# Spreading the plain units over the chains of a seven-product matrix product, with other lead times for its loads and sums

## The chip, the cores and the metric

The kernel runs on one core of a Trainium2 chip. The core has a matrix engine (TensorE, in profiles PE, with PEld for its weight loads), a vector engine (VectorE, DVE), a scalar engine (ScalarE, ACT), a general one (GpSimd, POOL) and a queue engine (SyncE, SP) that only issues transfers. POOL issues transfers too, here those that add to what is already in on-chip memory. The engines run side by side and wait for one another through semaphores; each takes its own instructions in order.

The metric is the device time of one execution in microseconds (us), the median of three runs.

## The reference

One layer of a hybrid decoder for 512 tokens of width 1024 in fp32: three token mixers, merged by gates, and then a gated MLP with a causal depthwise convolution of width 3, with a residual, and a last RMSNorm. What matters here is the MLP, of inner width 3072:

```python
h2 = rms_norm(x, norm_ffn[l])
up = causal_dwconv(h2 @ w_up[l], ffn_conv_w[l], ffn_conv_b[l])
gate_h, val_h = jnp.split(up, 2, axis=-1)
x = x + (jax.nn.gelu(gate_h, approximate=True) * val_h) @ w_down[l]
...
return rms_norm(x, final_norm)
```

## The kernel before

**fp32 by three passes.** Each operand of a large product is split into a high part, rounded to the matrix engine's fp32r (ACT, L97), and a low part, the rest (DVE, L98). `mm3` (L100) multiplies high by high, high by low and low by high into the same PSUM bank. So each tile of weights and activations is first "split", on ACT and then on DVE, before PE may use it.

**The MLP's tiles.** The inner width is 24 blocks of 128 channels. For each block there is a gate half and a value half. A *plain unit* of the up product (`up_units`) makes one half of one block for all 512 tokens: 24 matmuls. It fetches 512 KB of `w_up` into a buffer of the tag `raw` (three of them, `NRAW`), splits it into buffers `whi` and `wlo` (four of each, `NWB`), multiplies, and evacuates the bank: L1172 on ACT and L1174 twice on DVE are the convolution, and behind the second half of a block L1186 and L1187 are gelu and the product of both halves (`up_mix`). The result `acts[i]` takes a slot of the pool `apool`, tag `s`, which has 51 slots (`NSLOT`) of 2 KB a partition for everything of this size. I call the two units of block 21 up21.0 and up21.1. Some other blocks go through `up_fast`, which is not touched.

**The down product.** Blocks 0 to 19 are multiplied with `w_down` in five groups p of four blocks, each as a product of 2 x 2 parts, by seven products in place of eight (`down_fast`, which builds the operands, and `seven`, which builds the work). The seven products, called a1, a2, c1, c2, b1, b2 and b3, run in this order, each with five *chain units* p = 0 to 4 of 12 matmuls (b2.3 is the unit p = 3 of b2). They need sums of weight parts and of activation parts:

- *Weights.* The part B11 is loaded once per group (two transfers of 256 KB by SP, L296, into two slots of tag `s`) for a1, and stays. Before c1, b1 and b3 another part (B12, B22, B21) is added to it in place, by two accumulating transfers on POOL (L301; I call them sums). b2 loads B12 into two more slots (L296), and adds B22 to it (L301). a2 and c2 use B21 and B22 as they are, through `raw` (`direct`, L305). Each unit's weights are then split into `whi` and `wlo`.
- *Activations.* DVE forms the sums for b1, c1 and c2 (`sum2`, `sum1`, `sum4`; L1317, L1323, L1328). `act_ready` splits a unit's activations into two slots of tag `s`.
- *Banks.* a1, b1, b2 and b3 accumulate in the same two banks, one after the other, and c1 and c2 in two others. At the end of each of these products DVE adds the banks to the residual (`put`, L1341: two instructions), and the next product of the same banks can only go on behind that.

Blocks 20 to 23 are multiplied plainly in the end (`down_units` with `wdown2`: 96 matmuls, with activations split by the steps `halves`), and the last norm follows.

**What sets the order.** `unit`, `made_unit` and `step` put units and steps on a list. Each unit has preparations with a lead, in units: a preparation with lead m is called just ahead of the unit m places earlier (`emit`, L183). The lead counts all units, chain and plain alike; splits have 2 (`AHEAD`). In `seven`, the sums of c1, b1 and b3 have the lead `more`, the loads of b2 the first number of `late`, and its sums the second:

```python
"b1": ("B11", [(more, lambda p: add("B11", "B22", p))]),
"b2": ("B12", [(late[0], lambda p: load("B12", p)), (late[1], lambda p: add("B12", "B22", p))]),
"b3": ("B11", [(more, lambda p: add("B11", "B21", p))]),
```

A planner then makes each engine's queue from this program: an instruction can go ahead of earlier ones of the program when its data and a buffer are there.

When the down product begins, seven plain units are left (up20.1 to up23.1: `us`). The order is written out in the last lines of the kernel: up20.1, a1.0 to a1.4, up21.0, a2.0 to a2.4, up21.1, c1.0 to c1.2, up22.0, c1.3, c1.4, c2.0, c2.1, up22.1, c2.2 to c2.4, up23.0, b1.0 to b1.3, up23.1, b1.4, b2.0 to b2.4, b3.0 to b3.4, with the four `halves` steps in front of b3.0 to b3.3.

Of the kernel before, what the change touches and what calls it, by code (L numbers as in the profile page):

```python
# [34 lines left out]
NF = FF // P  # L35
# [22 lines left out]
def trunk(ctx: ExitStack, tc: tile.TileContext, x, xT, mem, memT, par, wdecay, wch, wv, wg, wmk,  # L58
# [17 lines left out]
    def fslot(shape=(P, S)):  # L76
        return apool.tile(list(shape), F32, tag="s", name=nm("f"))

    def rslot(shape=(P, S)):
        return apool.tile(list(shape), F32R, tag="s", name=nm("r"))  # L80
# [14 lines left out]
    def split(hi, lo, src, eng=None):  # L95

        nc.scalar.activation(hi, src, AF.Copy)  # L97
        return (eng or nc.vector).tensor_tensor(out=lo, in0=src, in1=hi.bitcast(F32), op=ALU.subtract)  # L98
# [34 lines left out]
    def unit(dram, n, fn, parts=1):  # L133

        w = {}
        i = sum(1 for k, *_ in prog if k == "unit")

        def ready():
            w["w"] = fetch(dram, n, parts)
            for h in behind.get(i, ()):  # L140
                h()
        prog.append(("unit", [(AHEAD, ready)], lambda: fn(w["w"])))

    def made_unit(pre, fn):

        prog.append(("unit", pre, fn))

    def step(fn):
        prog.append(("step", [], fn))
# [197 lines left out]
    def run(*parts):  # L347

        for p in parts:
            if isinstance(p, tuple):  # L350
                unit(*p)
            else:
                for v in p:
                    made_unit(*v) if isinstance(v, tuple) else step(v)
# [742 lines left out]
    def gain_rows(src):  # L1097
        for j in range(2):
            gb[j] = fslot()
            with tc.issue_after(loads[-1].ins):  # L1100
                nc.sync.dma_start(gb[j], src[:, j * HB:(j + 1) * HB])

    msq, queue, late = {}, [], []
# [86 lines left out]
    def up_units(tiles, keep, early=0):  # L1190

        us = []
        first = []
        for n in range(2 * len(tiles)):
            i, half = tiles[n // 2], n % 2
            if n < early:

                def fn(w, n=n):
                    first.append((w, channel_major(w, KD, h2k, 0, S // 2)))
                    if n != 1:  # L1200
                        norm2_flip(2 + n // 2)
                    if n == early - 1:
                        for m, (v, ps) in enumerate(first):
                            channel_major(v, KD, h2k, S // 2, S, ps)
                            up_done(ps, tiles[m // 2], m % 2, keep)
                us.append((wup[NF * half + i], D, fn, 2))
            else:
                us.append((wup[NF * half + i], D,
                           lambda w, i=i, half=half: up_done(channel_major(w, KD, h2k), i, half, keep)))
        return us  # L1210
# [92 lines left out]
    def down_fast(np):  # L1303

        a_in, a_sp = {}, {}
        sub, add = ALU.subtract, ALU.add

        def parts(p):

            for key, odd, r in (("a1", 0, 0), ("b2", 0, 1), ("a2", 1, 0), ("b3", 1, 1)):  # L1310
                a_in[key, p] = [acts[4 * p + 2 * j + odd][:, r * HT:(r + 1) * HT] for j in range(2)]


        def sum2(p):
            s2 = a_in["b1", p] = fslot((P, 2, HT))
            for j in range(2):
                nc.vector.scalar_tensor_tensor(out=s2[:, j, :], in0=a_in["b2", p][j], scalar=-1.0, in1=a_in["b3", p][j],  # L1317
                                               op0=ALU.mult, op1=sub)

        def sum1(p):  # L1320
            a_in["c1", p] = a_in["a1", p]
            for j, a in enumerate(a_in["a1", p]):
                nc.vector.tensor_tensor(out=a, in0=a, in1=a_in["b1", p][:, j, :], op=add)  # L1323

        def sum4(p):
            a_in["c2", p] = a_in["a2", p]
            for j, a in enumerate(a_in["a2", p]):
                nc.vector.tensor_tensor(out=a, in0=a, in1=a_in["b1", p][:, j, :], op=add)  # L1328

        def act_ready(key, p):  # L1330
            hi, lo = rslot((P, 2, HT)), rslot((P, 2, HT))
            a = a_in[key, p]
            if isinstance(a, list):
                for j in range(2):
                    split(hi[:, j, :], lo[:, j, :], a[j])
            else:
                split(hi, lo, a)
            a_sp[key, p] = hi, lo

        def put(t, c, src, op=ALU.add):  # L1340
            nc.vector.tensor_tensor(out=x2[t][c], in0=x2[t][c], in1=src, op=op)  # L1341

        def read(key, i, ps):
            put(*{"a1": (i, 0, ps), "a2": (i, 0, ps), "c1": (2 + i, 1, ps), "c2": (i, 1, ps), "b1": (i, 1, ps, sub),
                  "b2": (2 + i, 1, ps, sub), "b3": (2 + i, 0, ps)}[key])

        pre = {k: [(2, lambda p, k=k: act_ready(k, p))] for k in ("a1", "a2", "c1", "c2", "b1", "b2", "b3")}

        pre["a1"].append((3, parts))
        pre["a2"].append((np - 1, sum2))  # L1350
        pre["c1"].append((np - 1, sum1))
        pre["c2"].append((np, sum4))
        return seven(lambda q, p: wdown[p, int(q[1]) - 1, int(q[2]) - 1], HB, np,
                     lambda key, p, j, i: tuple(a[:, j, i * P:(i + 1) * P] for a in a_sp[key, p]), pre, read,
                     chained=True, more=8, late=(8, 5))

    def final_left(t):

# [40 lines left out]
    def halves(i):  # L1399
        a, acts[i] = acts[i], (rslot(), rslot())  # L1400
        split(*acts[i], a)

    us = up_units((0, 1, 2), whole, 3)
# [4 lines left out]
    us = up_units((5, 8, 11, 14, 17, 19), whole) + up_units(range(20, NF), whole)  # L1408
    ahead = None
    for i, even in zip((3, 4, 6, 7, 9, 10, 12, 13, 15, 16, 18), (None, 0, 2, None, 4, 6, 8, 10, 12, 14, None)):  # L1410
# [7 lines left out]
        ahead = f  # L1418
    run([ahead["b1"]], us.pop(0), [lambda: down_s3(16)], [ahead["b2"]], us.pop(0), [ahead["b3"]], [lambda: down_s3(18)])
    down, n = down_fast(5), 0  # L1420
    for m, u in zip((5, 5, 3, 4, 3, 4), us):
        run(u, down[n:n + m])
        n += m
    run(us[-1], down[n:n + 6])
    for i, u in zip(range(20, NF), down[n + 6:]):
        run([lambda i=i: halves(i)], [u])
    run(down[n + 10:])
    step(lambda: gain_rows(gfin))
    weave(down_units(wdown2, lambda k: acts[20 + k], final, None, final_left, 2), [])

# [92 lines left out]
```

## Time and profile before

| | us |
|---|---|
| median of 3 runs | 929.19 (928.91 to 930.28) |
| the profiled execution | 931.17 |
| its span, first to last instruction | 929.1 |
| PE busy | 909.7 |
| DVE busy | 662.1 |
| ACT busy | 537.7 |
| POOL busy | 145.6 |

The profile is of one execution. Its page lists each engine's busy time, the span in 40 slices, the chain of work that ended last, and the costliest groups of instructions by line, tile names and shapes. Other views of the same trace group the instructions by window, list who waited for whom, or give the instructions in order of time. Times in them are counted from the span's start. The down product of blocks 0 to 19 lies at about 763 to 900 us, the plain one of blocks 20 to 23 behind it, up to 922. "POOL f L301" is an issue of a sum, "SPq L296" one of a load, and "ACT whi L97" and "DVE wlo L98" are the two halves of a weight split.

### The profile page before, as it was taken

The numbers are of one execution on the slowest core, as the hardware profiler recorded it, in microseconds if no ns is written. First come the engines' busy times: TensorE is split into PE (matmuls) and PEld (weight loads), VectorE is DVE, ScalarE is ACT, GpSimd is POOL, SyncE is SP. The second block draws the span as 40 slices with busy tenths as digits, with TensorE's granted clock in tenths as the row PEclk, the third lists the DMA queues.
The fourth block names the chain that finished last, engine by engine and source line by source line (L and its number), as shares of the span: only waits on it lengthen the run. The fifth ranks groups of instructions, "written<-read, shape, count | busy, mean of one in ns | idle before, by whom it ended". The sixth has DMA issues, their size and how long they took to land.

```text
span 929.1 us, 13271 instructions
## 1 busy us (share of the span) xinstructions
PE 909.7 (98%) x4786; PEld 790.8 (85%) x4786; DVE 662.1 (71%) x1195; ACT 537.7 (58%) x936; POOL 145.6 (16%) x188
## 2 busy tenths in 40 slices
PE   9999999999999999999999999999999999999796
PEld 7899788888889998888888798999999988888585
DVE  6996855665688567747776668778787789876665
ACT  7775655685855468484534455665565565455544
POOL 0010000000233430330000000222222121306102
PEclk9999999999999999999999999999999999999799
DMA  7446223213468783321157324767676766869602
GB/s 249 141 137 206 91 87 100 88 45 116 115 162 184 173 208 117 111 85 52 52 170 244 112 58 114 183 141 200 141 200 137 175 142 163 166 186 233 137 23 91
DMA packets 55505, 128.55 MB, mean 138 GB/s; under 512 B 6624, under 2 KB 14480, under 8 KB 55440
## 3 DMA queue, kind: packets, MB, share of 16 engines
q1 hardware_dynamic: 37088, 94.99, 31.2%
q0 software_dynamic: 18208, 32.46, 20.5%
q8 instruction: 37, 0.61, 0.3%
q10 hardware_dynamic: 144, 0.26, 0.1%
q14 instruction: 28, 0.23, 0.1%
HBM read 123.23 MB, written 3.67 MB: 137 GB/s over the span
## 4 chain that ended last, share of the span: by engine, by line
PE 77%; issue 7%; DMA 7%; DVE 5%; ACT 2%; POOL 2%; SPq 0%; DVEq 0%; POOLq 0%; ACTq 0%
PE mm L104 65%; PE sm L104 7%; DMA f<-in_wdown 3%; DMA f<-in_wv 2%; PE mm L439 2%; DMA raw<-in_wup 2%; POOL f L301 2%; DVE wlo L98 1%; DVE r L98 1%; ACT r L97 0%; PE sm L999 0%; ACT whi L97 0%; PE sm L986 0%; PE sm L1013 0%; DMA raw<-in_wch 0%
## 5 line engine op out<-in xcount | busy, mean ns | idle before, releaser
L98 DVE TENSOR_TENSOR wlo<-raw,whi 128x1024 fp32r<-128x1024 f32 (+3 forms) x132 | 145.3, 1104 | 86.1 <-ACT whi L97 49.2
L97 ACT ACTIVATE whi<-raw 128x1024 fp32r<-128x1024 f32 (+3 forms) x132 | 125.1, 953 | 127.5 <-PE mm L104 93.2
L104 PE MATMUL mm<-whi,r 128*128 128x512 f32 (+2 forms) x568 | 170.7, 376 | 6.3 <-DVE m L1341 6.3
L104 PEld LDWEIGHTS mm<-whi,r 128*128 128x128 f32 x568 | 106.9, 190 | 22.8 <-ACT whi L97 6.7
L104 PE MATMUL mm<-hh,whi 128*128 128x512 f32 x288 | 113.4, 394 | 0.0
L104 PE MATMUL mm<-hl,whi 128*128 128x512 f32 x288 | 112.8, 391 | 0.0
L97 ACT ACTIVATE r<-f 128x512 fp32r<-128x512 f32 (+3 forms) x184 | 91.4, 541 | 34.4 <-DMA f<-in_wup 32.4
L104 PE MATMUL mm<-wlo,r 128*128 128x512 f32 (+2 forms) x284 | 106.8, 376 | 0.5 <-DVE wlo L98 0.5
L98 DVE TENSOR_TENSOR r<-f,r 128x512 fp32r<-128x512 f32 (+3 forms) x184 | 102.2, 585 | 4.8 <-ACT r L97 4.4
L104 PE MATMUL mm<-r,whi 128*128 128x512 f32 (+1 forms) x432 | 94.2, 367 | 0.0
L104 PEld LDWEIGHTS mm<-r,whi 128*128 128x128 f32 x432 | 75.2, 189 | 13.1
L1259 POOL DMA_DIRECT2D f<-in_wup x44 | 38.6, 979 | 285.0 <-PE sm L1150 131.7
L97 ACT ACTIVATE whi<-f 128x512 fp32r<-128x512 f32 (+2 forms) x90 | 48.4, 579 | 57.7 <-PE mm L104 41.1
L104 PE MATMUL mm<-r,r 128*128 128x256 f32 (+2 forms) x456 | 81.5, 329 | 0.0
L104 PEld LDWEIGHTS mm<-r,r 128*128 128x128 f32 (+1 forms) x456 | 68.7, 187 | 9.7 <-ACT r L97 0.2
L98 DVE TENSOR_TENSOR wlo<-f,whi 128x512 fp32r<-128x512 f32 (+2 forms) x90 | 53.6, 630 | 31.9 <-ACT whi L97 27.8
L104 PE MATMUL mm<-h2l,whi 128*128 128x512 f32 x184 | 71.8, 390 | 0.0
L104 PE MATMUL mm<-h2h,whi 128*128 128x512 f32 x184 | 71.6, 390 | 0.0
L104 PE MATMUL mm<-hh,wlo 128*128 128x512 f32 x288 | 71.4, 389 | 0.0
L104 PEld LDWEIGHTS mm<-hh,wlo 128*128 128x128 f32 x288 | 54.0, 188 | 11.2
L104 PEld LDWEIGHTS mm<-hh,whi 128*128 128x128 f32 x288 | 54.1, 188 | 10.8
L104 PEld LDWEIGHTS mm<-hl,whi 128*128 128x128 f32 x288 | 54.1, 188 | 10.8
(258 smaller groups left out, 1624.5 us busy)
## 6 DMA issues: line engine op xcount, KB each, us to landing
raw<-in_wch SPq DMA_DIRECT2D x39, 512.0 KB, 3.3
raw<-in_wup SPq DMA_DIRECT2D x26, 512.0 KB, 4.4
f<-in_wup SPq DMA_DIRECT2D x44, 256.0 KB, 5.4
f<-in_wup POOLq DMA_DIRECT2D x44, 256.0 KB, 5.5
f<-in_wdown POOLq DMA_DIRECT2D x40, 256.0 KB, 7.4
raw<-in_wbr SPq DMA_DIRECT2D x24, 384.0 KB, 3.1
raw<-in_wdown SPq DMA_DIRECT2D x14, 512.0 KB, 4.2
f<-in_wdown SPq DMA_DIRECT2D x20, 256.0 KB, 5.1
```

The source lines that it names most:

```text
L97: nc.scalar.activation(hi, src, AF.Copy)
L98: return (eng or nc.vector).tensor_tensor(out=lo, in0=src, in1=hi.bitcast(F32), op=ALU.subtract)
L104: nc.tensor.matmul(ps, lhsT=l, rhs=r, start=first and i == 0, stop=last and i == len(seq) - 1, skip_group_check=more)
L301: nc.gpsimd.dma_start(raw[to, p][j], src(q, p)[:, j, :], accum_op=ALU.add)
L439: nc.tensor.matmul(ps[u], lhsT=w(a, u, k), rhs=xs["r"][k][j], start=k == 0 and i < n, stop=k == KD - 1 and i >= len(seq) - n)
L1259: nc.gpsimd.dma_start(raw[q], src(more), accum_op=ALU.add)
```

## The change

Two things change. In `down_fast`'s call of `seven`, `more` goes from 8 to 6 and `late` from (8, 5) to (9, 6): the sums of c1, b1 and b3 are asked for six units ahead and no longer eight, b2's loads nine and no longer eight, and its sums six and no longer five. By places in the list, all of b2's sums now stand ahead of b3's first.

And the order of the last lines is another: one plain unit ahead of each chain of five. It is up20.1, a1, up21.0, a2, up21.1, c1, up22.0, c2, up22.1, b1, up23.0, b2, up23.1, b3, with the four `halves` steps behind b3.1 to b3.4.

```diff
                      lambda key, p, j, i: tuple(a[:, j, i * P:(i + 1) * P] for a in a_sp[key, p]), pre, read,
-                     chained=True, more=8, late=(8, 5))
+                     chained=True, more=6, late=(9, 6))
...
     down, n = down_fast(5), 0
-    for m, u in zip((5, 5, 3, 4, 3, 4), us):
-        run(u, down[n:n + m])
-        n += m
-    run(us[-1], down[n:n + 6])
-    for i, u in zip(range(20, NF), down[n + 6:]):
-        run([lambda i=i: halves(i)], [u])
-    run(down[n + 10:])
+    for i, u in enumerate(us):
+        run(u, down[5 * i:5 * i + 5 if u is not us[-1] else -4])
+    for i, u in zip(range(20, NF), down[-4:]):
+        run([u], [lambda i=i: halves(i)])
     step(lambda: gain_rows(gfin))
```

## The prediction

> **What bounds it now.** I read the page first, then the matrix engine's waits, then a table by windows, then the chain and the timelines around the one hole.
>
> ```profile
> span 929.1 us, 13271 instructions
> ...
> PE 909.7 (98%) x4786; PEld 790.8 (85%) x4786; DVE 662.1 (71%) x1195; ACT 537.7 (58%) x936; POOL 145.6 (16%) x188
> ...
> PEclk9999999999999999999999999999999999999799
> ```
>
> PE is busy all the time, except for one slice of the forty (the 7). The reader is to see that other engines count only where they stop PE. PE's waits and the table by windows (PE, weight loads, DVE, ACT, POOL, granted clock, DMA share, GB/s) show one place:
>
> ```profile
> PE mm L104 <- DVE m L1341: 6.3, 1, 6.3
> PE sm L623 <- ACT f L610: 1.4, 1, 1.4
> ```
> ```profile
> 863.40:869.80 6.40, 0.10 (x1) 0.02 (x1) 4.77 (x9) 4.54 (x11) 0.41 (x1) 0.67 1.13 205
> 869.80:875.50 5.70, 5.69 (x14) 4.44 (x15) 3.67 (x9) 1.18 (x5) 0.00 (x0) 0.50 0.29 52
> ...
> 900.10:921.90 21.80, 21.75 (x96) 17.66 (x95) 9.54 (x27) 8.93 (x22) 5.17 (x4) 1.00 0.12 45
> ```
>
> PE stands for 6.3 us, and then it runs for 5.7 us at half its clock. Undisturbed, 96 matmuls take 21.75 us, 0.2266 each; so a chain unit (12 matmuls) is 2.72 us and a plain unit (24) 5.44 us. Why does it stand? The chain, DVE's timeline and PE's (start, length, what):
>
> ```profile
> 850.98 14.05 DMA f<-in_wdown
> 865.04 0.02 issue
> 865.06 0.64 ACT whi L97
> ...
> 865.72 0.69 DVE wlo L98
> ...
> 868.98 0.69 DVE m L1341
> 869.67 0.14 issue
> 869.81 52.05 PE mm L104 x216
> ```
> ```profile
> 856.04 1.29 DVE L98 TENSOR_TENSOR wlo<-f,whi 128x512 fp32r<-128x512 f32 x2 [1.21 <-ACT whi L97]
> 864.50 0.69 DVE L98 TENSOR_TENSOR wlo<-f,whi 128x512 fp32r<-128x512 f32 x1 [7.17 <-ACT whi L97]
> ```
> ```profile
> 854.72 0.62 PE L104 MATMUL mm<-whi,r 128*128 128x512 f32 x2
> 855.17 0.39 PE L104 MATMUL mm<-h2h,whi 128*128 128x512 f32 x1
> ...
> 860.62 0.39 PE L104 MATMUL mm<-whi,r 128*128 128x512 f32 x1
> ```
>
> At 855.17 the last plain unit, up23.1, begins; at 860.62 b1.4, which ends at 863.3. b2.0 accumulates in b1's banks, so it needs b1 read first (L1341). That read stands in DVE's queue behind up23.1's evacuation, and this behind a weight split (864.50) that waits for a sum issued on POOL at 850.98 and landed at 865.0, after 14 us. By counting the weight splits on ACT after up23.1's I take it for b2.2's. So the cause is a late sum for the b2 chain, in a queue ahead of an urgent read, with no plain unit between b1.4 and b2.0 to cover it.
>
> Where the sum's lateness comes from (SP's and POOL's queues):
>
> ```profile
> 811.43 8.52 SPq L305 DMA_DIRECT2D raw<-in_wdown  x3
> 822.31 3.78 SPq L166 DMA_DIRECT2D raw<-in_wup  x2
> 828.48 4.05 SPq L166 DMA_DIRECT2D raw<-in_wdown  x2
> 832.58 16.13 SPq L296 DMA_DIRECT2D f<-in_wdown  x10
> ```
> ```profile
> 808.79 1.76 POOL L301 DMA_DIRECT2D f<-in_wdown  x2 [0.79 <-DVE wlo L98]
> 837.11 8.01 POOL L301 DMA_DIRECT2D f<-in_wdown  x9 [26.56 <-DVE r L98]
> ...
> 862.95 0.87 POOL L301 DMA_DIRECT2D f<-in_wdown  x1 [0.21 <-issue]
> ```
>
> ```profile
> 872.00:874.00 2.00, 2.00 (x6) 0.50 0.02 3
> ```
>
> POOL issues no sum between 810.6 and 837.1; then the 20 sums of b2 and b3 go in one burst, with b2's ten loads of 832.6 to 848.7 among them, and the DMA engines are idle again only from 872 (share 0.02 in the row of the finer windows). Why are the loads not earlier? ACT's timeline and two rows of DVE's:
>
> ```profile
> 804.70 0.71 ACT L97 ACTIVATE r<-f 128x256 fp32r<-128x256 f32 x2
> ...
> 814.52 0.78 ACT L1172 ACTIVATE f<-mm,prm 128x512 f32<-128x512 f32 x1 [0.75 <-PE mm L104]
> 815.20 1.33 ACT L97 ACTIVATE r<-f 128x256 fp32r<-128x256 f32 x4
> ...
> 830.90 0.78 ACT L1172 ACTIVATE f<-mm,prm 128x512 f32<-128x512 f32 x1 [0.75 <-PE mm L104]
> 831.58 1.24 ACT L97 ACTIVATE r<-f 128x256 fp32r<-128x256 f32 x3
> ```
> ```profile
> 798.87 2.76 DVE L1328 TENSOR_TENSOR f<-f,f 128x256 f32<-128x256 f32 x8
> ```
>
> c2's activations are summed by 801.6, yet the splits of c2.0 and c2.1 come only at 815.2, right behind up22.0's evacuation (814.52), and that of c2.4 at 831.58, right behind up22.1's (830.90). The loads at 832.58 fit the same rule. I read from this, as an inference, that slots of the 51-slot pool are given out in the order of the program: what is asked for after a plain unit's evacuation waits for that evacuation. Under this rule the lead numbers matter by which side of an evacuation they put a load on.
>
> **The change part by part.** No instruction is added or taken away: the same 35 chain units, 7 plain units, 4 halves steps and as many transfers. So the sum is waits alone.
>
> *Order.* Before, the units after up21.1 are c1.0-2, up22.0, c1.3-4, c2.0-1, up22.1, c2.2-4, up23.0, b1.0-3, up23.1, b1.4, b2, b3. After: c1, up22.0, c2, up22.1, b1, up23.0, b2, up23.1, b3. The row below has up21.1's evacuation start at 800.92, so c1.0 starts at 800.7:
>
> ```profile
> 800.92 0.78 ACT L1172 ACTIVATE f<-mm,prm 128x512 f32<-128x512 f32 x1 [0.75 <-PE mm L104]
> ```
>
> By units of 2.72 and 5.44, without a hole: c1 to 814.3, up22.0 to 819.8, c2 to 833.4, up22.1 to 838.8, b1 to 852.4, up23.0 to 857.9, b2 to 871.5, up23.1 to 876.9, b3 to 890.5. Each chained bank's read (1.3 us for two) now has a plain unit behind it, so a read may be 5.4 us late for nothing. In return b1 and b2 are due 5.4 us sooner than an undisturbed before would have them; c1.3-4 are too.
>
> *c1 without up22.0 in it.* DVE is full here:
>
> ```profile
> 784.00:809.00 25.00, 25.00 (x112) 20.71 (x111) 25.00 (x53) 14.55 (x29) 7.21 (x9) 1.00 0.73 160
> ```
> ```profile
> 805.27 1.28 DVE L98 TENSOR_TENSOR wlo<-f,whi 128x512 fp32r<-128x512 f32 x2
> 806.48 1.42 DVE L98 TENSOR_TENSOR r<-f,r 128x256 fp32r<-128x256 f32 x4
> 807.82 1.28 DVE L98 TENSOR_TENSOR wlo<-f,whi 128x512 fp32r<-128x512 f32 x2
> ```
>
> Even on the old timetable c1.3's splits end by 807.9 and c1.4's by 809.1; the new starts are 808.9 and 811.6. Bounds: nothing if ready, 5.4 us if the splits stay tied to the unit that moved; I take nothing, nearest to these rows.
>
> *Loads of b2 nine units ahead (8 before).* Counted in units, b2.0, b2.1 and b2.2 are now asked for at c2.3, c2.4 and at up22.1 before its evacuation; before, all five were asked for behind the evacuation of up22.1. Behind up22.0's evacuation (819.8) I count as held: 20 activation tiles, 10 of B11, 5 of the b1 sums, 3 of up20 to up22, and 2 per split unit, 10 for c2: 48 of 51. So b2.0's two loads fit at about 820 to 823, b2.1 and b2.2 as c2's units give slots back, by 829. b2.3 and b2.4 come behind up22.1's evacuation, 840 to 843. That is some 12 us sooner than 832.6 for the first and 5 us sooner than 848.7 for the last. SP's cost is the same ten issues; queued behind one that waits for a slot are raw fetches, which run far ahead of PE (that at 828.48 is for the last product, which PE reaches at 900.1).
>
> *Sums six units ahead (8), b2's too (5), b3's behind b2's.* c1 and b1 sums wait for the split of the same tile, not for their place, so I cost 8 to 6 at nothing; at its place a sum has at least five chain units and a plain one, 19.0 us, against the 14.05 us of the worst shown. b2's can start near 825, so that they have landed by about 850, b2.3 and b2.4 by about 860; b2.2 is due at 863.3. Even if the two last take the 14 us of the burst, 847 + 14 + 1.4 for the split is 862.4, before 866.0 where b2.3 is due. The cover is thus 3 us or more.
>
> A rule that speaks against this: the Trainium skill, DMA: Bandwidth & Descriptors, Issuing engines are not separate DMA queues, says that transfers from all queues share the same 16 engines, so an earlier issue makes none of them faster. By it the burst of some 40 us (832.6 to 872) would, begun at 820.5, end at 860.5, still ahead of b2.4; the sum would be the same.
>
> *b3 and the halves.* up23.1's evacuation now falls at 877, and behind it stand the splits for b3.2-4, four halves and two weight splits, about 12 us of DVE before 890.5. Bounds: 0 to 1.5 us; I take 0.
>
> **Sum.** The hole gives 6.3 us. The 216 matmuls behind it took 52.05 us and need 216 x 0.2266 = 48.95: the half clock gives 3.1. Together 9.4 us. PE would end at 912.5 instead of 921.9; the 7.2 us behind it stay. The profiled execution took 931.17 us (span 929.1 and 2.1 around it): 921.8. The median of the runs is 2.0 lower, 929.19: **919.8 us**.
>
> **Rivals.** (1) *The order on POOL does not change*: b3's sums, ready as soon as b1's splits are, still go ahead of b2.2's, which land at 865.0 as now. b2.2 then starts at 866.4 instead of 863.3: 3.1 us lost, and up to 3.1 of half clock. Gain 3.2 to 6.3: 922.9 to 926.0. For it: POOL serves what is ready, and b3's sums are ready at about 830. Against: the loads are sooner by more than that. The Trainium skill, TensorE: Matmul & The Clock Gate, Why this matters for your kernels, has the clock fall for gaps over about 3 us; here a 6.3 us gap did it; by that rule a gap of 3.1 us is at the edge, and without the clock's loss this rival gives 922.9.
> (2) *Small holes* in the crowded places (c1.3, b2.2, b3): 1 to 3 us, 921 to 923; gaps of that size elsewhere (1.4 us) left the clock whole.
> (3) *Slower: b2's loads stay behind up22.1's evacuation*, because no slot is free before it. That evacuation moves from 830.9 to 838.8, 7.9 us later. b2.2 then lands at 872.9, starts at 874.3 instead of 863.3, 11.0 lost, and 3.1 at half clock: 919.8 + 14.1 = 933.9. It decides from a landing of b2.2 at about 868, where it eats the 9.4. For it: slots are tight, my count leaves 3. Against: the count.
> (4) *The hole only moves*, within 0.2% of before: landings of about 868.
>
> **How the numbers follow.** Forecast 0.70 (919.0 to 921.0), small holes 0.08, old order 0.10, within 0.2% 0.04, slower 0.08. 0.2% is about what this measurement tells from no change. Faster 0.88, same 0.04, slower 0.08. For 8 in 10 the range takes the forecast, the small holes and the better half of rival 1: 918.9 to 924.5.
>
> **What would show it.** Right: no PE wait on L1341, PE's clock 9 throughout, the first L296 loads of b2 at 820 to 823, POOL at work before 837, span near 919.7. Wrong: first b2 load after 838 (rival 3); b3's sums ahead of b2.2's and a hole at 863 (rival 1); a PE wait on DVE at 809 to 812 or 880 to 890 (rival 2).

## The result, and the profile after

| | before | after |
|---|---|---|
| median | 929.06 us (928.91 to 930.28, 4 runs) | 920.78 us (919.39 to 921.84, 4 runs) |
| ratio of the two | | 0.9907 [0.989, 0.9924] |
| span of the profiled execution | 929.1 | 919.2 |
| its time | 931.17 | 921.2 |

The change makes the kernel some 8.3 us faster. First the page of the changed kernel (span, busy time, granted clock in 40 slices), its matrix engine's waits (us in all, times, longest) and the last of PE in its chain:

```profile
span 919.2 us, 13268 instructions
PE 907.2 (99%) x4786; PEld 788.8 (86%) x4786; DVE 662.0 (72%) x1195; ACT 537.2 (58%) x936; POOL 145.4 (16%) x188
PEclk9999999999999999999999999999999999999998
```
```profile
PE sm L1150 <- DVE f L1132: 1.5, 1, 1.5
PE sm L211 <- DVE warm L207: 1.1, 1, 1.1
```
```profile
741.58 170.33 PE mm L104 x768
```

The wait on L1341 is gone from the list, the 7 in the clock's row is a 9, and one unbroken run of 768 matmuls now stands at the chain's end, where before the chain went through a sum, two splits and an evacuation. The work is the same.

To compare kernels I use the **stage**: the time from a1's first matmul to the end of the span. These rows of PE's timeline, of the kernel before and of the changed one, show its start:

```profile
762.64 0.39 PE L104 MATMUL mm<-whi,r 128*128 128x512 f32 x1
```
```profile
762.13 0.39 PE L104 MATMUL mm<-whi,r 128*128 128x512 f32 x1
```

So the stage was 166.5 us and is 157.0. The difference, 9.4, is all that changed; the other 0.5 us of the two spans lies ahead of a1, which nothing here touches, and where executions of one kernel differ by a few microseconds (a1 began between 759.4 and 763.6 in the profiled runs of this study). The stage is therefore a finer measure than the time.

SP's and POOL's queues after (start, length, what):

```profile
820.76 0.33 SPq L166 DMA_DIRECT2D raw<-in_wup  x1
821.14 0.90 SPq L296 DMA_DIRECT2D f<-in_wdown  x2
824.55 0.33 SPq L166 DMA_DIRECT2D raw<-in_wup  x1
824.92 1.78 SPq L296 DMA_DIRECT2D f<-in_wdown  x2
827.24 0.33 SPq L166 DMA_DIRECT2D raw<-in_wdown  x1
827.62 15.09 SPq L296 DMA_DIRECT2D f<-in_wdown  x6
```
```profile
827.17 1.76 POOL L301 DMA_DIRECT2D f<-in_wdown  x2 [19.50 <-issue]
829.26 5.33 POOL L301 DMA_DIRECT2D f<-in_wdown  x6 [0.33 <-DVE wlo L98]
...
853.92 0.87 POOL L301 DMA_DIRECT2D f<-in_wdown  x1 [1.94 <-DVE wlo L98]
```

b2.0's loads start at 821.1 (832.6 before) and POOL's burst of 20 sums at 827.2 (837.1 before). Its last sum is issued 9 us sooner than before (853.9 for 862.95). What the burst still does is seen on ACT and DVE at b2:

```profile
857.35 0.63 ACT L97 ACTIVATE whi<-f 128x512 fp32r<-128x512 f32 x1 [4.11 <-DMA f<-in_wdown]
860.30 0.63 ACT L97 ACTIVATE whi<-f 128x512 fp32r<-128x512 f32 x1 [2.32 <-DMA f<-in_wdown]
860.84 0.76 ACT L1172 ACTIVATE f<-mm,prm 128x512 f32<-128x512 f32 x1
```
```profile
861.63 0.75 DVE L1174 SCALAR_TENSOR_TENSOR f<-mm,prm,f 128x511 f32<-128x511 f32 x1
862.30 0.41 DVE L98 TENSOR_TENSOR r<-f,r 128x256 fp32r<-128x256 f32 x1
...
863.29 1.08 DVE L98 TENSOR_TENSOR r<-f,r 128x256 fp32r<-128x256 f32 x3
```

ACT waits for b2.3's two sums (until 857.2 and 860.3), and behind them in its queue stand up23.0's evacuation, whose bank was full at 857.5, and b2.2's activation splits. The latter end on DVE at 862.7 and 863.7; PE begins b2.2 at 862.8, with the high parts, and needs the low ones within the next microsecond. So PE doesn't stand, but the margin is a few tenths.

### The profile page after: what moved, and what is told of

Same layout as the page of the kernel before. It is cut to its first block, busy times and chain, and to the rows that moved or that the text cites. A ratio compares the mean times of both kernels' runs of the same rounds, so it can differ in the third digit from the quotient of the medians.

```text
span 919.2 us, 13268 instructions
## 1 busy us (share of the span) xinstructions
PE 907.2 (99%) x4786; PEld 788.8 (86%) x4786; DVE 662.0 (72%) x1195; ACT 537.2 (58%) x936; POOL 145.4 (16%) x188
## 4 chain that ended last, share of the span: by engine, by line
PE 88%; DVE 5%; DMA 3%; ACT 2%; issue 1%; SPq 0%; POOL 0%; DVEq 0%; POOLq 0%; ACTq 0%
PE mm L104 77%; PE sm L104 7%; DMA f<-in_wv 2%; PE mm L439 2%; DVE wlo L98 1%; DVE r L98 1%; DMA raw<-in_wch 0%; DVE f L395 0%; PE sm L999 0%; DMA raw<-in_wup 0%; ACT r L97 0%; ACT whi L97 0%; PE sm L986 0%; PE sm L1013 0%; DVE f L813 0%
## 5 line engine op out<-in xcount | busy, mean ns | idle before, releaser
L104 PE MATMUL mm<-whi,r 128*128 128x512 f32 (+2 forms) x568 | 168.2, 372 | 0.0
```

The source lines that it names most:

```text
L104: nc.tensor.matmul(ps, lhsT=l, rhs=r, start=first and i == 0, stop=last and i == len(seq) - 1, skip_group_check=more)
```

## Experiments

All expectations are of the time, the stage or the hole (a stand of PE). Stages and holes are of one profiled execution each:

| kernel | stage | holes in it | median | ratio to before |
|---|---|---|---|---|
| before | 166.5 | 6.3 | 929.06 | |
| the change | 157.0 | none | 920.78 | 0.9907 [0.989, 0.9924] |
| order_only | 158.4 | 0.45, 0.38 | 921.21 | 0.9909 [0.9889, 0.9928] |
| leads_only | 161.0 | 2.0 | 924.85 | 0.994 [0.9922, 0.9957] |
| loads_late | 161.8 | 2.9 | 923.73 | 0.994 [0.9921, 0.9959] |
| b3_behind | 157.0 | none | 920.19 | 0.9893 [0.9875, 0.991] |
| cover_b1 | 164.0 | 2.9, 1.5 | 927.4 | 0.9978 [0.9965, 0.9991] |
| before_hold | 159.3 | 2.0 | 924.49 | 0.9937 [0.9912, 0.9962] |
| more8 | 157.4 | none | 920.55 | 0.9898 [0.9877, 0.9919] |
| slots53 | 165.3 | 5.9 | 929.83 (one run) | |
| change_again | 158.2 | 0.23, 0.38 | 920.27 | 0.9909 [0.9895, 0.9923] |
| b3_behind_again | 157.0 | none | 920.39 | 0.991 [0.9896, 0.9924] |
| raw_behind | 169.3 | 9.3 | 932.5 | 1.0026 [1.0012, 1.0039] |

### The order alone, and the leads alone

**order_only**, the changed kernel with the old leads:

```diff
-                     chained=True, more=6, late=(9, 6))
+                     chained=True, more=8, late=(8, 5))
```

> The new order of units with the old leads (more=8, late=(8, 5)). Theory (the hole came from b2's sums landing late; the leads decide on which side of up22.1's evacuation b2's loads stand): only b2.0 and b2.1 load ahead of it, b2.2 to b2.4 at about 840; their sums land at about 856 to 864 where they are due at 861 to 867; no hole or one under 3 us, 919.5 to 923. Rival (the even spread of the plain units alone is what counts): as the change itself, 920 to 921.5, and no nearer to a hole. Rival (the leads count most): a hole of 5 us or more, 926 to 930.

**leads_only**, the kernel before with the new leads:

```diff
-                     chained=True, more=8, late=(8, 5))
+                     chained=True, more=6, late=(9, 6))
```

> The old order of units with the new leads (more=6, late=(9, 6)). Theory: b2's loads stay behind up22.1's evacuation, at 832 to 848 as before, but b2.2's sums go ahead of some of b3's on POOL, so they land 3 to 6 us sooner than 865.0; the hole behind b1.4 shrinks to 0 to 3 us and with it the half clock: 920 to 925. Rival (the spread alone counts): the hole stays at 6 us, 927 to 930.

In these profiles the order alone gives 8.0 of the 9.4 us, the leads alone 5.5: the two don't add up. PE's timeline of order_only shows what it leaves:

```profile
861.85 0.50 PE L104 MATMUL mm<-whi,r 128*128 128x512 f32 x1 [0.45 <-ACT r L97]
863.65 0.73 PE L104 MATMUL mm<-whi,r 128*128 128x512 f32 x2 [0.38 <-DVE r L98]
```

Both stands wait for b2.2's activation splits, first the high parts (ACT) and then the low ones (DVE); it is the place where the changed kernel passes by a few tenths. One thing went otherwise than expected: b2.2's loads, asked for behind up22.1's evacuation, went out at 828.3 and 828.8, some 8 us ahead of it (837.0 in this run), and not at about 840.

With the leads alone, SP issues b2's loads as late as before (from 832.0), but POOL's planned order has b2's first sums ahead of most of b3's. ACT's timeline, PE's waits and a table by windows (as in the prediction) of leads_only:

```profile
858.43 1.17 ACT L97 ACTIVATE whi<-f 128x512 fp32r<-128x512 f32 x2 [2.47 <-PE mm L104]
```
```profile
PE mm L104 <- DVE m L1341: 2.0, 1, 2.0
```
```profile
864.00:866.00 2.00, 1.07 (x4) 0.87 (x5) 2.00 (x5) 0.56 (x1) 0.00 (x0) 0.96 1.13 205
866.00:868.00 2.00, 2.00 (x6) 1.60 (x5) 1.39 (x4) 1.39 (x5) 0.00 (x0) 0.50 1.13 204
```

b2.2's weight split (858.43) waits for a buffer that PE frees, no longer for a sum. Yet PE stands for 2.0 us on L1341, and then runs at half clock.

### The sums in time, without the new order

**before_hold**, the kernel before, b3's sums held behind b2's on POOL:

```diff
-        raw, w, banks = {}, {}, {}
+        raw, w, banks, sums = {}, {}, {}, {}
...
             for j in range(2):
-                nc.gpsimd.dma_start(raw[to, p][j], src(q, p)[:, j, :], accum_op=ALU.add)
+                with tc.issue_after(sums["B12"].ins) if chained and q == "B21" else ExitStack():
+                    sums[to] = nc.gpsimd.dma_start(raw[to, p][j], src(q, p)[:, j, :], accum_op=ALU.add)
```

> The kernel before, order of units and leads as they were, with each of b3's sums held on POOL until the b2 sum that the program has asked for by then is issued: b2.0 to b2.2 go first, then b3.0, then b2.3. Theory (b3's sums in front are what makes b2.2 late): loads still at 832 to 848, b2.2's sums land by 853 and no longer at 865, no hole behind b1.4, a1's start to the end 157 to 158.5 us, 919.5 to 922. Rival (the burst as a whole is too late, whatever its order): hole of 3 us or more, 923 to 929.

PE's waits, DVE's timeline and the table by windows of before_hold (its lines are one further down):

```profile
PE mm L104 <- DVE m L1342: 2.0, 1, 2.0
```
```profile
861.81 1.29 DVE L98 TENSOR_TENSOR wlo<-f,whi 128x512 fp32r<-128x512 f32 x2 [3.54 <-ACT whi L97]
863.02 0.74 DVE L1175 SCALAR_TENSOR_TENSOR f<-mm,prm,f 128x511 f32<-128x511 f32 x1
...
865.61 1.28 DVE L1342 TENSOR_TENSOR m<-m,mm 128x512 f32<-128x512 f32 x2
```
```profile
864.00:866.00 2.00, 0.43 (x2) 0.01 (x1) 2.00 (x5) 1.53 (x4) 2.00 (x3) 1.00 1.09 189
866.00:868.00 2.00, 1.57 (x7) 1.34 (x8) 2.00 (x5) 0.85 (x3) 0.54 (x1) 1.00 1.12 203
```

With the sums in time, a hole of 2.0 us is left: the read of b1 at 865.61 stands behind b2's split and the rest of up23.1's evacuation (863.02 to 865.6), and DVE is busy throughout. That is what the missing plain unit between b1.4 and b2.0 costs by itself. The late sum is worth the other 4.3 of the 6.3 us. I had expected both to go with the sum.

### The plain unit behind b1, with the sums still late

**cover_b1**, the kernel before, up23.1 between b1.4 and b2.0:

```diff
-    for m, u in zip((5, 5, 3, 4, 3, 4), us):
+    for m, u in zip((5, 5, 3, 4, 3, 5), us):
...
-    run(us[-1], down[n:n + 6])
+    run(us[-1], down[n:n + 5])
...
```

> The kernel before with one unit moved: up23.1 runs behind b1.4 and no longer ahead of it; old leads, rest of the order as before. Theory (the hole was b1's read caught in DVE's queue behind b2.2's late split; a plain unit between b1.4 and b2.0 covers it): b2.2's sums land at about 866 as before, PE needs them at 867 to 869; the wait on L1341 goes, a hole of 0 to 2 us is left at b2.2, the stretch from a1's start to the end is 157 to 160 us (166.5 before, 157.1 in the changed kernel), 920 to 923. Rival (the landing alone decides, no matter what covers it): a hole of 4 us or more, 925 to 929.

PE's waits and ACT's timeline of cover_b1:

```profile
PE mm L104 <- ACT r L97: 2.9, 1, 2.9
PE mm L104 <- DVE m L1341: 1.5, 1, 1.5
```
```profile
864.51 0.63 ACT L97 ACTIVATE whi<-f 128x512 fp32r<-128x512 f32 x1 [6.54 <-DMA f<-in_wdown]
...
869.58 0.63 ACT L97 ACTIVATE whi<-f 128x512 fp32r<-128x512 f32 x1 [0.65 <-DMA f<-in_wdown]
870.11 0.76 ACT L1172 ACTIVATE f<-mm,prm 128x512 f32<-128x512 f32 x1
870.77 1.32 ACT L97 ACTIVATE r<-f 128x256 fp32r<-128x256 f32 x4
```

Four weight splits wait for sums one after the other, from 858 to 870, and behind them stand the evacuation and b2.2's activation splits. So the wait goes from L1341 to the activations: PE stands for 2.9 us in front of b2.2, until 871.2. The other 1.5 us end at 883.1, where b3.0 waits for the read of b2: no plain unit stands between those two. The cover alone gives 2.5 us of stage. My theory, that the cover would be nearly enough, fell: with the sums still late, most of the time stays lost.

### b2's loads late in the new order

**loads_late**, the changed kernel, b2's loads six units ahead, its sums five:

```diff
-                     chained=True, more=6, late=(9, 6))
+                     chained=True, more=6, late=(6, 5))
```

> The changed kernel with late=(6, 5) in place of (9, 6): all of b2's loads are asked for behind up22.1's evacuation, which ends its unit at 838.5. Rival 3 of the prediction: the first load of b2 at 839 or later, a hole in b2 of some 11 us and half clock, 930 to 936. Theory of late sums without the burst (b3's sums are through by then): landings at 851 to 866, holes of 0 to 4 us, 920 to 927. If the loads' place is of no account: 920 to 921.5.

SP's timeline, PE's waits and the table by windows of loads_late:

```profile
827.41 17.47 SPq L296 DMA_DIRECT2D f<-in_wdown  x10
```
```profile
PE mm L104 <- DVE m L1341: 2.9, 1, 2.9
```
```profile
856.00:860.00 4.00, 1.24 (x6) 0.70 (x4) 2.03 (x5) 1.28 (x3) 1.75 (x2) 1.00 1.11 242
860.00:862.00 2.00, 1.89 (x5) 1.54 (x6) 1.51 (x3) 1.24 (x2) 0.00 (x0) 0.56 1.13 205
```

A lead of six places all of b2's loads behind up22.1's evacuation (838.2 in this run). Four of them went out at 827.4 to 830.1 all the same, 8 to 11 us ahead of it; the other six at 840.5 to 844.6. A hole of 2.9 us comes back, 4.7 us of stage with the half clock. The sums' lead of five isn't the reason, since order_only has it too. So the first number of `late` matters, but the prediction's rule for when a load may start doesn't hold.

### Slots, or SP's queue

**slots53**, the kernel before with two more slots:

```diff
-NSLOT = 51
+NSLOT = 53
```

> The kernel before with 53 slots in place of 51 in the pool of tag s. Theory of the prediction (slots are given out in the order of the program, so b2's loads wait for what stands ahead of them and not for a free slot): b2's loads at 832 to 833 as before, the same hole of about 6 us, 928 to 931. Rival (there are too few slots): the loads go out 3 us or more sooner, the hole shrinks, below 927.

```profile
832.71 15.03 SPq L296 DMA_DIRECT2D f<-in_wdown  x10
```

Two more slots leave the loads where they were (832.71). In every run of this study b2's first loads go out 0.4 us behind a fetch into `raw`. Before, the last of these fetches, at 832.2, is one of the last product's, and DVE's timeline shows the raw split ending just then (830.95 + 1.23 = 832.18):

```profile
830.95 1.23 DVE L98 TENSOR_TENSOR wlo<-raw,whi 128x1024 fp32r<-128x1024 f32 x1 [2.50 <-PE mm L104]
```

`raw` has three buffers, so the loads may have stood behind a fetch that waited for one. So:

**raw_behind**, the kernel before; the last product's fetches behind b2.2's loads on SP:

```diff
-        loads.append(nc.sync.dma_start(raw, dram))
+        with tc.issue_after(wait_b2[2].ins) if 4 in wait_b2 else ExitStack():
+            loads.append(nc.sync.dma_start(raw, dram))
...
+            if chained and q == "B12":
+                wait_b2[p] = loads[-1]
```

> The kernel before, with one thing else: on SP the last product's two raw fetches stand behind b2.2's loads and no longer ahead of b2.0's. Theory SP: b2.0's loads were not held by slots but by the second of these fetches, which waits for a raw buffer, so for a weight split that ends at 832.2; they go out now right behind the fetch of up23.1 (825.8), at 826 to 827, some 6 us sooner. Rival (the prediction's rule): the slots come behind up22.1's evacuation of 830.9, and the loads stay at 832 to 833. For the time both expect nothing: POOL's first sums of the burst are b3.0's, which wait until 837 for b1.0's split, and b2.2's stand 13th and 14th, landing at 1.3 us apiece; so a hole of 5.5 to 6.5 us on L1341 and 928 to 931 us. If the time of the loads alone were the cause, the hole would shrink by some 6 us, and the time be 920 to 922.

SP's and POOL's timelines, PE's waits and the chain of raw_behind:

```profile
822.33 3.79 SPq L169 DMA_DIRECT2D raw<-in_wup  x2
826.17 22.69 SPq L299 DMA_DIRECT2D f<-in_wdown  x10
848.91 1.66 SPq L169 DMA_DIRECT2D raw<-in_wdown  x3
```
```profile
837.14 8.00 POOL L306 DMA_DIRECT2D f<-in_wdown  x9 [26.61 <-DVE r L98]
```
```profile
PE mm L104 <- ACT r L97: 9.3, 1, 9.3
```
```profile
842.77 14.32 DMA f<-in_wdown
857.37 14.51 DMA f<-in_wdown
871.91 0.63 ACT whi L97
```

b2.0's loads now start at 826.17, 6.4 us sooner: SP's queue held them, as the theory said. (b2.1's and b2.2's stay at 833.2 and 836.7; what holds those is open.) It brings nothing: POOL's burst begins at 837.14 as before, with b3's sums. And it costs 2.8 us of stage, which neither theory had: three fetches of 512 KB now start at 848.9 to 850.1, in the middle of the burst, where before there was one (849.6), and b2.2's second sum lands at 868.1 and not at 865.0. Behind it on DVE the read of b1 comes at 872.0 and not at 869.0. PE goes on 0.1 us after the first bank's read, as before; the view names an activation split that ended at the same time, and that stood on ACT behind a weight split for a later sum, the one which the chain has landing at 871.9. So the hole is as long as the sums are late. That the fetches beside them made them later is the likely reading; the run moved the loads too.

### `more`, and b3's sums

**more8**, the changed kernel, the sums of c1, b1 and b3 eight units ahead:

```diff
-                     chained=True, more=6, late=(9, 6))
+                     chained=True, more=8, late=(9, 6))
```

> The changed kernel with more=8 in place of 6, late=(9, 6) kept. Theory (a sum waits for its tile's split, not for its place, so more counts for nothing, and late's first number is what took order_only's small hole away): POOL's and SP's order as in the changed kernel, a1's start to the end 157.0 to 157.5, 919.5 to 921.5. Rival (six in place of eight is needed): a hole, 921.5 or more.

No difference, and POOL's planned order is the changed kernel's own. b3_behind is the changed kernel with the hold of before_hold:

> The changed kernel with b3's sums held on POOL until b2's last sum is issued. Theory (in the changed kernel b2's activation split behind up23.0's evacuation comes within 0.5 us of PE's need, because the ACT and DVE queues wait for b2.3's sums that stand behind b3's; runs that lose this race explain the spread of 919.4 to 921.8): b2.2's sums land by 846 and b2.3's by 856, the wait on ACT ahead of up23.0's evacuation goes, spread under 1 us, median 919.0 to 920.3. Rival (the spread is something else): 920 to 921.5 and as wide as before.

> The changed kernel itself once more, on the chip of the run beside it. From a1's first matmul to the end of the span 157.0 us, no wait of PE on L1341, clock at full; time 919.4 to 922, as a1 begins between 759.4 and 763.6.

> Theory (the order of the sums on POOL no longer costs anything once the hold fits): the same 157.0 us from a1 to the end as the changed kernel, and a time within 0.2% of it on the same chip. Rival (the margin of b2.2's split, a few tenths in the changed kernel, is lost in some runs): 0.5 to 1.5 us faster than the changed kernel on the same chip.

PE's timeline of change_again:

```profile
860.63 0.50 PE L104 MATMUL mm<-whi,r 128*128 128x512 f32 x1 [0.23 <-ACT r L97]
862.44 0.73 PE L104 MATMUL mm<-whi,r 128*128 128x512 f32 x2 [0.38 <-DVE r L98]
```

The changed kernel's own stage was 157.0 once and 158.2 the other time, when b2's activation splits came too late by tenths. With the hold, b3's sums go behind b2's, b2.3's last sum lands at 843.6 (in b3_behind) and not at 860.3, and the stage was 157.0 twice. In the times that can't be seen: 0.991 beside 0.9909 on the same chip. Nor is the spread of the runs smaller, as I had thought it might be (918.19 to 922.76, and 919.54 to 922.89). So I don't call b3_behind a better kernel.

## Why the prediction was right, and where it wasn't

The forecast of 919.8 us was met within 1.0 us: 920.78, and 920.27 when run again.

- **The sum: right.** 6.3 us of hole and 3.1 of half clock, 9.4; the stage lost 9.4. The difference of the medians is smaller, 8.3, and the interval of the ratio, 7.1 to 10.2 us, holds both.
- **The cause: right, but it has two parts.** It was a late sum in a queue ahead of an urgent read, with no plain unit to cover it; before_hold and cover_b1 part them. Without the late sum 2.0 us of hole stay; with a plain unit behind b1 but the sum still late, 2.9 us stay in front of b2.2 and 1.5 come up in front of b3. The new order mends both: a plain unit stands in front of each chain, and b1 comes some 6 us sooner (838.3 for 844.3), and with it the splits that b3's sums wait for on POOL (the first of them goes at 829.3 for 837.1).
- **When the loads start: right numbers for b2.0 to b2.2, wrong rule.** 820 to 829 was forecast for these three, and 821.1 to 828.1 came. But the step that slots are given out in program order, so that a load asked for behind an evacuation waits for it, fell in loads_late and order_only, and in the changed kernel itself: b2.3's loads, forecast for 840 to 843 behind up22.1's evacuation, went out at 832.6 and 833.0, ahead of it (838.5). What does hold the loads back, besides the fetches, is open. The sentence that the raw fetches in front "run far ahead of PE" fell too: one of them held b2.0's loads (raw_behind), and the changed kernel's loads too come 0.4 us behind such fetches.
- **`more` at nothing: right** (more8). **b3's sums behind b2's: not so.** On POOL they still stand between b2's, and those of b3.0 even ahead of b2.1's. It cost nothing that the time shows.
- **A cover of 3 us or more: wrong.** b2.0 to b2.2 are loaded and summed by 849.2 as forecast (850), but b2.3's sums land at 857.2 and 860.3 and b2.4's at 861.6 and 862.8. The step reckoned each sum with its own due time; it left out that ACT takes them in turn, so that a sum for b2.3 holds back b2.2's activations. What is left is tenths, and in change_again they weren't enough. That the hole closed whole in the first profile, as the sum had it, was luck by that much.
- **The rivals.** The old order on POOL (922.9 to 926.0) came in part, as b3.0's sums still go ahead of b2.1's, but without its price. Small holes came in change_again, at about 1.2 us of stage. For the slower one, loads behind up22.1's evacuation, 933.9 wasn't seen: with a lead that asks for all of them behind it, loads_late took 923.7, but four of the ten went out ahead of it even so. That a fetch in the wrong place can make the kernel slower is shown by raw_behind.
- **The leads** weren't priced apart from the order. With the new order the old leads give 0.9909 beside 0.9907, no difference that the times show. Nor do the stages show one: 158.4, beside 157.0 and 158.2 for the two runs of the changed kernel. So what the new numbers add to the new order isn't shown; with the old order they bring 5.5 us (leads_only).

## What to carry to other kernels

When PE stands on a read, follow each queue in front of the read to its own head: a single late transfer blocked ACT, DVE and PE in turn, and making a different transfer earlier brought nothing. A plain unit between two chains that share banks is cover for the read, but it helps little (2.5 of 9.4 us here) while late sums hold up ACT. And an issue taken out of a queue's way comes down elsewhere: the moved fetches of 512 KB went with sums that landed 3 us later.

## What the hardware showed that I had not expected

**The clock after a gap of 2.0 us** went both ways: half in leads_only (0.50 at 866 to 868 us in its windows above), full in before_hold (1.00 in the same window). After 2.9 us in loads_late it fell to 0.56. After the 1.5 us in cover_b1 it stayed at 1.00 (883 to 885). The prediction had taken gaps of 1 to 3 us as harmless. The Trainium skill, TensorE: Matmul & The Clock Gate, Why this matters for your kernels, gives gaps over about 3 us as the limit; here 2.0 us was enough in one run, and that measurement decides. Why the same gap left the clock whole in the other is open.

**Sums in a crowd.** A sum of 256 KB landed 4.3 to 4.7 us after its issue when it was the first of a burst (before, leads_only, before_hold, raw_behind), and mostly 10 to 14 us after it within one, at about 1.3 us apiece. The longest of before took 14.3 us. In raw_behind, with the three fetches beside them, it was up to 16.8 us. The rule of the Trainium skill that the prediction weighed (DMA: Bandwidth & Descriptors, Issuing engines are not separate DMA queues: all queues share 16 engines) agrees with that: with more fetches issued by SP in flight, sums issued by POOL landed later.
